# The second float32r part of each weight unit made by an accumulating DMA instead of a subtraction, in a two-layer hybrid decoder trunk

## The chip, the cores and the metric

The kernel runs on one core of a Trainium2 chip. The metric is the time of one execution on the device in microseconds (us), as the median of several runs. The engines go by their short names in the profile: PE (TensorE matmuls; PEld its weight loads), DVE (VectorE), ACT (ScalarE), POOL (GpSimd) and SP (SyncE, which here only issues DMAs). A DMA issued by an engine goes into that engine's queue, and the core's 16 DMA engines carry it out.

## The reference

Two decoder layers over 512 tokens of 1024 features, all in float32. Each layer is a half-step SwiGLU feed-forward, a token mixer, and a second half-step feed-forward; each of these sublayers has an RMS norm before and after it. The mixer of the first layer is a diagonal complex state-space model (S5), that of the second a convolution module of 31 taps.

```
for i in range(DEPTH):                       # DEPTH = 2
    h = swiglu(rmsnorm(x, norm_pre[i, 0]), w1[i, 0], w3[i, 0], w2[i, 0])
    x = x + 0.5 * rmsnorm(h, norm_post[i, 0])
    h = rmsnorm(x, norm_pre[i, 1])
    h = s5_mixer(h, ...) if i == 0 else conv_mixer(h, ...)
    x = x + rmsnorm(h, norm_post[i, 1])
    h = swiglu(rmsnorm(x, norm_pre[i, 2]), w1[i, 1], w3[i, 1], w2[i, 1])
    x = x + 0.5 * rmsnorm(h, norm_post[i, 2])
# swiglu(h) = (silu(h @ w1) * (h @ w3)) @ w2, inner width 2816
```

## The kernel before

**The arithmetic.** PE multiplies in float32r, which keeps fewer bits than float32. So every operand is held as two float32r parts: a first part (the value rounded) and a second part (what the rounding left). A product takes three matmuls: first x first, first x second, second x first (`mm3`, lines 105, 106 and 107, in this order, with the weight's part as the stationary operand). Line 107 is the only one that reads the weight's second part.

**The stream of weights.** All weights are cut into units of 128 x 1024 (512 KB), eight 128 x 128 blocks each: 44 + 22 units for each of four feed-forward sublayers, 24 for each mixer, 312 in all. A unit goes three steps. `w_dma` (line 86) loads it on SP's queue into one of three buffers called raw. `want(n)` splits all units up to n: ACT rounds raw into the first part `hi` (line 97, a cast), and DVE subtracts that from raw into the second part `lo` (line 98). In some places `lo_engine` hands that subtraction to POOL. Then `mm3` uses the unit. 310 units are split by `want`; the first two are split by halves in `start` (lines 188 and 189).

**Buffers and order.** `hi` and `lo` are pages: 39 buffers of 128 x 1024 (tag `pg`), shared with activations and tables. The order of instructions on each engine is the order in which the program emits them; each engine runs its own list in order, and an instruction waits there for the data and buffers that it needs. So the place of a `want` sets how far ahead of its matmuls a unit is split.

- In a feed-forward sublayer (`ffn`) a step takes two units. Step m asks for units up to `u0 + 2m + 4` (`FFN_AHEAD`), behind its own matmuls in the program. At its start, after the entry, `want(u0 + 6)` splits the fifth to seventh unit.
- In a sublayer's last product (`proj`) each unit, when begun, asks for the unit two further on (line 273). Near its end `want(un + 2)` splits the next sublayer's first three units, and while the norm of the first half of the tokens is made, POOL subtracts the fourth, `want(un + 3)`.
- The entry (`entry_step`) runs the next sublayer's first four units, feature tile by feature tile, by halves of the tokens, as the residual and its two parts come from DVE (lines 322, 326, 164) and ACT (lines 154 to 159); POOL adds up the squares (line 160).

**Work beside it.** During the first feed-forward and the next sublayers the tables of the state-space model are made in small portions (queues D, E, Q, K, T, P) on DVE, POOL and ACT. The state-space sublayer and the convolution run mostly on DVE, with a share of POOL and ACT; in the convolution DVE does its taps at line 1037.

Of the kernel before, what the change touches and what calls it, by code (L numbers as in the profile page):

```python
# [7 lines left out]
F32 = mybir.dt.float32  # L8
F32R = mybir.dt.float32r
AF = mybir.ActivationFunctionType  # L10
ALU = mybir.AluOpType
# [3 lines left out]
NF = 22  # L15
EPS_SUM = 1024e-6

# columns of the packed vector input
V_PRE, V_POST, V_BGLU, V_CBIN, V_DWB, V_LNG, V_LNB, V_CBOUT, V_DW = 0, 48, 96, 104, 120, 128, 136, 144, 152
CONV_W = 31  # L20
ND = 9
# taps of a feature tile that the vector engine takes (GpSimd the others), None: the tensor engine
C_TAPS = (31, 0, 21, None, None, None, 20, 16)
NL = 2
S5_ORDER = ("sktwdopcgl", "sktwdopcgl", "stwdopcgkl", "skwtdopcgl", "skwtdopcgl", "skwtdolpcg", "skwtdopcgl", "skwtdopcgl", "skwtdopcgl")
# [14 lines left out]
def trunk(ctx: ExitStack, tc: tile.TileContext, h, plan):  # L40
# [24 lines left out]
    def psum():  # L65
        return psp.tile([P, T], F32, tag="ps", name=nm("ps"))

# [1 line left out]
    x = cpool.tile([P, NK, T], F32, name="x")  # L69
    vec = cpool.tile([P, h["vec"].shape[1]], F32, name="vec")  # L70
    gsc = cpool.tile([P, 96], F32, name="gsc")
# [1 line left out]
    eps = cpool.tile([P, 1], F32, name="eps")  # L73
    lng = cpool.tile([P, 8], F32, name="lng")

# [1 line left out]
    units = [h[name][i] for name, i in plan["units"]]  # L77
    NU = len(units)
    raws, halves = {}, {}
# [10 lines left out]
    def want(n):  # L90
        while ptr["split"] <= min(n, NU - 1):
            u = ptr["split"]
            w_dma(u)
            r = raws.pop(u)
            hi, lo = page(), page()
            hv, lv = hi.rearrange("p a b -> p (a b)"), lo.rearrange("p a b -> p (a b)")
            ACT.copy(hv, r)  # L97
            lo_engine[0].tensor_tensor(lv, r, hv.bitcast(F32), op=ALU.subtract)  # L98
            halves[u] = tuple(v.rearrange("p (k m) -> p k m", m=P) for v in (hv, lv))
            ptr["split"] += 1  # L100
            w_dma(u + 3)
# [4 lines left out]
        PE.matmul(out, lhsT=hi[:, s, :], rhs=xl, start=False, stop=False)  # L106
        PE.matmul(out, lhsT=lo[:, s, :], rhs=xh, start=False, stop=stop)  # L107

# [1 line left out]
    def stat(acc):  # L110
        ps = psum()
        PE.matmul(ps[:, : acc.shape[1]], lhsT=ones, rhs=acc, start=True, stop=True)  # L112
# [37 lines left out]
    HALVES = (slice(0, T // 2), slice(T // 2, T))  # L150

    def split_hi(k, cs, xn, pre, acc2):
        """x[k] times the gain, the first part; the squares of x into acc2."""
        ACT.activation(xn[k][:, 0, cs], x[:, k, cs], AF.Copy, scale=gsc[:, pre + k : pre + k + 1])  # L154
        if k == 0:
            ACT.activation(acc2[:, cs], x[:, k, cs], AF.Square)
        else:
            sq = tmp()
            ACT.activation(sq[:, cs], x[:, k, cs], AF.Square)  # L159
            POOL.tensor_tensor(acc2[:, cs], acc2[:, cs], sq[:, cs], op=ALU.add)  # L160
# [9 lines left out]
            mm3(ps4[j][:, cs], u0 + j, k, xn[k][:, 0, cs], xn[k][:, 1, cs], k == 0, k == NK - 1)  # L170

    def start(pre):
        """The first sublayer's entry."""
        xn = [page() for _ in range(NK)]
        acc2 = stat_tile()
        ps4 = [psum() for _ in range(4)]
        for i in range(11):
            PE.matmul(ps4[2][:, :P], lhsT=ones, rhs=ones, start=True, stop=True)
        pieces = []
        for u in range(2):  # L180
            hi, lo = (flat(page()) for _ in range(2))
            pieces.append((raws.pop(u), hi, lo))
            halves[u] = tuple(v.rearrange("p (k m) -> p k m", m=P) for v in (hi, lo))
        ptr["split"] = 2

        def split_part(u, n):
            r, hi, lo = (v[:, T * n : T * n + T] for v in pieces[u])
            ACT.copy(hi, r)
            DVE.tensor_tensor(lo, r, hi.bitcast(F32), op=ALU.subtract)

        def part_hi(k):
            ACT.activation(xn[k][:, 0, :], x[:, k, :], AF.Copy, scale=gsc[:, pre + k : pre + k + 1])  # L192

        def squares(k):
            if k == 0:
                ACT.activation(acc2, x[:, k, :], AF.Square)
            else:
                sq = tmp()
                ACT.activation(sq, x[:, k, :], AF.Square)
                POOL.tensor_tensor(acc2, acc2, sq, op=ALU.add)  # L200

        for k in range(NK):
            part_hi(k)
            split_lo(k, FULL, xn, pre)
            if k in (0, 4):
                split_part(0, k // 4)
                split_part(1, k // 4)
            entry_step(k, FULL, xn, 0, ps4, (0, 1))
            if k:
                squares(k - 1)  # L210
        want(2)
        squares(NK - 1)
        want(3)
        for j in (2, 3):
            for k in range(NK):
                entry_step(k, FULL, xn, 0, ps4, (j,))
        return {"xn": xn, "ps": ps4, "acc2": acc2, "u": 0}
# [4 lines left out]
        rsqrt(ps, e["y"])  # L222

    def proj(u0, nk, rhs, post, nl, pre, xn, bias=None, lead=None):
        """The sublayer's last product, its norm, the residual, and the next one's entry."""
        acc, acc2 = stat_tile(), stat_tile()
        hp = [page(F32) for _ in range(4)]
        hs = [hp[m // 2][:, m % 2, :] for m in range(NK)]
# [40 lines left out]
        for m in range(0 if lead is None else 4, NK - nl):  # L269
            ps = psum()  # L270
            for k in range(nk):
                if k == 0 or unit(m, k)[1] == 0:
                    want(min(unit(m, k)[0] + 2, un - 1))
                product(m, k, ps, FULL)
                if k == 1 and pend:
                    evac(*pend)
                    copy(*pend)
                if k % 8 == 4:
                    pump("P")
            pend = m, ps, FULL  # L280
# [18 lines left out]
        for i, (m, k) in enumerate((m, k) for m in last for k in range(nk)):  # L299
            if i == 5:  # L300
                sa = stat(acc[:, A])
                steps = rsqrt_steps(sa, y[:, A])
                if pre is not None:
                    lo_engine[0] = POOL
                    want(un + 3)
                    lo_engine[0] = DVE
                for f in steps:
                    f()
            if k == 0:
                psb[m] = psum()[:, :n]  # L310
            product(m, k, psb[m], B)
            if k == nk - 1 and m != NK - 1:
                evac(m, psb[m], B)
                copy(m, psb[m], B)
# [90 lines left out]
        evac(*pend)  # L405
        return proj(u0 + 2 * NF, NF, g, post, 1, pre, g[:NK])

# [1 line left out]
    # A pair is two groups (32 features, 128 complex states). Tokens go in chunks of four: the  # L409
    # stacked input of a chunk is (token in the chunk, feature of the pair) on the partitions.  # L410
    # Of each chunk come its own outputs (M) and its contribution to the state (P); the state
    # runs over the chunks in a frame that turns with it, and gives the rest of the outputs (Q).
    if any(k == "s5" for k, _ in plan["subs"]):
        drp = ctx.enter_context(tc.tile_pool(name="drp", bufs=1, space=bass.MemoryType.DRAM))
        tab_d = drp.tile([8, P, 3584], F32, name="tab_d")
# [3 lines left out]
        m4 = cpool.tile([P, 32], F32, name="m4")  # L419

    def s5_params(tb, F):
        """Per state: powers of abar and of the turn of a chunk, f abar^(3-t)."""
        scr = [page(F32).rearrange("p a (b n) -> p (a b) n", n=32) for _ in range(2)]
        ident = tmp()[:, :P]
        prm = tmp()[:, :96]
# [168 lines left out]
        bg["K"].append(turned())  # L594

    def s5_turn(tb):
        """exp(i phi c) of 128 chunks: 16 of them for all pairs, then tile by tile."""
        H = page(F32).rearrange("p r (q c) -> p r q c", c=16)
        w = page(F32).rearrange("p r (q c) -> p r q c", c=16)
        DVE.memset(H[:, 0, :, 0:1], 1.0)  # L600
# [24 lines left out]
            nc.sync.dma_start(out=tab_d[i, :, 2048:3072], in_=flat(E.rearrange("p r q c -> p r (q c)")))  # L625

    def s5_in():
        """P of the four pairs of each tile."""
        M, A, S = ALU.mult, ALU.add, ALU.subtract

        def load(i):
# [19 lines left out]
            yield  # L651

    def s5_ops(tb, F):
        """Q and M of the four pairs of each tile."""
        M, A, S = ALU.mult, ALU.add, ALU.subtract
        Fv = F.rearrange("p (t i r q) -> p t i r q", t=4, i=8, r=2)
        quads = lambda z: z.rearrange("p (q k g) -> p q k g", q=4, k=4)
# [85 lines left out]
    def s5(e, post, pre):  # L743
# [34 lines left out]
                    PE.matmul(b[:, j, :], lhsT=p[:, r, j, :], rhs=mu[:, 1, j, :], start=True, stop=True)  # L778

        def decay(i):  # L780
            """The coefficients of the scan: |abar|^4, and 0 where a pair begins."""
            if i <= 7:
                cf[i] = stat_tile()
                ACT.copy(quad(cf[i])[:, :, 1:], m4[:, 4 * i : 4 * i + 4].unsqueeze(2).to_broadcast([P, 4, n]))
                POOL.memset(quad(cf[i])[:, :, 0:1], 0.0)
# [102 lines left out]
        for s in range(9):  # L888
# [5 lines left out]
                g4.extend(psum() for _ in range(4))  # L894
            if s:
                back(s - 1)
            # transfers
            y_out(s - 2)
            load(s + 2, (0,))
            unstack(s + 2)  # L900
# [58 lines left out]
            u0 + 16, NK, z, post, NL, pre, [page() for _ in range(NK)], lead=lambda s: (FULL, s) if s < NK else None  # L959
        )  # L960

# [1 line left out]
    # Tiles of 128 features go different ways: on the vector engine (D), on the scalar engine and  # L963
    # GpSimd (G), on both (X), or on the tensor engine with banded operators (T).
    if any(k == "conv" for k, _ in plan["subs"]):
        drc = ctx.enter_context(tc.tile_pool(name="drc", bufs=1, space=bass.MemoryType.DRAM))
        z_d = drc.tile([8, P, T], F32, name="z_d")
# [2 lines left out]
    def conv(e, post, pre):  # L970
# [72 lines left out]
            yield  # L1043

        def diagonals():
            """Taps of the last tiles on the tensor engine, one diagonal matrix each."""
            for i, z, n, m in diags:
                op = flat(page(F32))
                nc.sync.dma_start(out=op[:, : m * P], in_=h["diag"][i - 6, :, n * P : (n + m) * P])
# [36 lines left out]
                total(i, a, b, DVE)  # L1086

        def shifted(i):
            """The tile less the shift, which the first tile's mean gives, and its squares."""
            if i == 0:  # L1090
                ps = psum()
                PE.matmul(ps, lhsT=ones, rhs=cs[0], start=True, stop=True)
                fin.append(lambda: shift(ps))
            fin.append(lambda: sums_of(i))
# [125 lines left out]
        while fin:  # L1220
            finish()
            add_sums()
        # layer norm, by halves of the tokens
        q, v, y0, w = tmp(), tmp(), tmp(), tmp()
        yp = page(F32)
        y, my = yp[:, 0, :], yp[:, 1, :]
# [48 lines left out]
            u0 + 16, NK, rhs, post, NL, pre, [page() for _ in range(NK)], bias=vec[:, V_CBOUT : V_CBOUT + 8], lead=lead  # L1275
        )

# [1 line left out]
    DVE.memset(ones, 1.0)  # L1279
    DVE.memset(eps, EPS_SUM)  # L1280
    nc.scalar.dma_start(out=vec[:, :48], in_=h["vec"][:, :48])
# [138 lines left out]
```

## Time and profile before

| what | value |
|---|---|
| three runs | 2028.13, 2026.94, 2029.37 us; median 2028.13 |
| span of the profiled execution | 2030.4 us; no other time is given for that execution |
| PE busy | 1887.8 us, 93% |
| DVE, ACT, POOL busy | 1267.2, 649.1, 389.4 us |
| mean granted clock of PE | 0.961 of full speed |
| subtractions of line 98 | 295 on DVE at 1261 ns, 15 on POOL at 2479 ns |
| moved by DMA | 229.17 MB, 34.0% of 16 engines' span on SP's queue |

Busy time is the time in which an engine had an instruction running; matmuls overlap, so a busy PE is not a PE at its peak. In a row of groups the two times behind the bar are the busy time of the whole group and the mean of one. "<-" behind an idle time names what ended it. PEclk is the clock that PE was granted, as a share of full speed. The bytes and the time of a DMA queue count what its packets took on the 16 DMA engines together.

### The profile page before, as it was taken

What the parts mean: (1) busy time and instruction counts of PE and PEld (TensorE: products, weight loads), DVE (VectorE), ACT (ScalarE), POOL (GpSimd) and SP (SyncE); (2) the same over time, 40 slices, a digit from 0 to 9 for tenths busy, and PEclk for the clock granted to TensorE, in tenths of its full rate; (3) what the DMA queues carried; (4) which work ended last, traced back from release to release, by engine and by line L of the source; (5) the groups of instructions that cost most, each with busy time, mean ns of one, the idle gap of its engine ahead of it and who ended that gap; (6) DMA issues with size and microseconds to landing.
All of it is one profiled execution on the core that took longest, in us unless ns stands there. A gap on an engine that the chain in (4) does not pass through costs nothing.

```text
span 2030.4 us, 23976 instructions
## 1 busy us (share of the span) xinstructions
PE 1887.8 (93%) x9226; PEld 1591.0 (78%) x9226; DVE 1267.2 (62%) x1828; ACT 649.1 (32%) x939; POOL 389.4 (19%) x401
## 2 busy tenths in 40 slices
PE   9978799998799999999999999999884799999997
PEld 7856588887678888888888888889772788888886
DVE  5998976758965754442376444237999786444324
ACT  4222232233224432222244222224433544232211
POOL 2446533034630100000020000002563120000000
PEclk9988899999899999999999999999996899999999
DMA  4234446846722232323224232231442024332231
GB/s 151 94 107 136 126 135 207 255 167 233 243 75 93 67 124 90 104 76 101 86 71 135 94 104 83 83 106 51 164 142 70 11 73 135 104 97 91 73 114 43
DMA packets 95811, 229.17 MB, mean 113 GB/s; under 512 B 25552, under 2 KB 39376, under 8 KB 95696
## 3 DMA queue, kind: packets, MB, share of 16 engines
q1 hardware_dynamic: 94400, 226.56, 34.0%
q8 instruction: 72, 1.18, 0.2%
q10 hardware_dynamic: 1296, 1.07, 0.2%
q14 instruction: 43, 0.35, 0.1%
HBM read 204.92 MB, written 22.68 MB: 112 GB/s over the span
## 4 chain that ended last, share of the span: by engine, by line
PE 73%; DVE 20%; issue 2%; ACT 2%; DMA 1%; SPq 0%; POOL 0%; DVEq 0%; ACTq 0%; POOLq 0%
PE ps L106 24%; PE ps L107 24%; PE ps L105 23%; DVE pg L1037 3%; DVE pg L98 2%; DVE pg L436 1%; DVE pg L803 1%; PE ps L1142 1%; DVE x L326 1%; DVE tmp L322 1%; DVE pg L164 1%; DVE pg L813 1%; DVE pg L705 1%; DVE pg L706 1%; PE ps L112 0%
## 5 line engine op out<-in xcount | busy, mean ns | idle before, releaser
L107 PE MATMUL ps<-pg,pg 128*128 128x512 f32 (+1 forms) x2808 | 1038.9, 370 | 27.8 <-DVE pg L98 24.7
L105 PE MATMUL ps<-pg,pg 128*128 128x512 f32 (+1 forms) x2808 | 1044.7, 372 | 14.6 <-ACT pg L154 5.0
L106 PE MATMUL ps<-pg,pg 128*128 128x512 f32 (+1 forms) x2808 | 1042.8, 371 | 13.2 <-DVE pg L164 10.0
L107 PEld LDWEIGHTS ps<-pg,pg 128*128 128x128 f32 x2808 | 537.6, 191 | 119.3 <-DVE pg L98 28.6
L106 PEld LDWEIGHTS ps<-pg,pg 128*128 128x128 f32 x2808 | 537.1, 191 | 112.2 <-DVE pg L164 17.4
L105 PEld LDWEIGHTS ps<-pg,pg 128*128 128x128 f32 x2808 | 537.3, 191 | 103.8 <-ACT pg L154 5.4
L98 DVE TENSOR_TENSOR pg<-raw,pg 128x1024 fp32r<-128x1024 f32 x295 | 360.9, 1261 | 84.5 <-ACT pg L97 51.9
L97 ACT CAST pg<-raw 128x1024 fp32r<-128x1024 f32 x310 | 310.1, 1047 | 113.2 <-DMA raw<-w 24.7
L98 POOL TENSOR_TENSOR pg<-raw,pg 128x1024 fp32r<-128x1024 f32 x15 | 36.9, 2479 | 875.3 <-ACT pg L97 875.3
L369 DVE TENSOR_TENSOR tmp<-ps,y 128x512 f32<-128x512 f32 x88 | 60.4, 686 | 217.0 <-PE ps L107 217.0
L248 DVE TENSOR_TENSOR acc<-acc,tmp 128x512 f32<-128x512 f32 (+1 forms) x50 | 36.6, 733 | 228.8 <-ACT tmp L243 228.5
L368 ACT ACTIVATE tmp<-tmp 128x512 f32<-128x512 f32 x88 | 55.6, 632 | 287.0 <-DVE tmp L367 287.0
L372 ACT CAST pg<-tmp 128x512 fp32r<-128x512 f32 x88 | 54.6, 621 | 290.1 <-DVE tmp L370 290.1
L243 ACT ACTIVATE tmp<-ps 128x512 f32<-128x512 f32 (+1 forms) x41 | 21.8, 533 | 267.4 <-PE ps L107 267.1
L1037 DVE SCALAR_TENSOR_TENSOR pg<-pg,vec,pg 128x512 f32<-128x512 f32 x80 | 105.7, 1389 | 0.0
L373 DVE TENSOR_TENSOR pg<-tmp,pg 128x512 fp32r<-128x512 f32 x88 | 61.2, 696 | 64.1 <-ACT pg L372 64.1
L1073 POOL TENSOR_TENSOR pg<-pg,pg 128x512 f32<-128x512 f32 x45 | 73.9, 1642 | 64.9 <-ACT pg L1071 62.0
L160 POOL TENSOR_TENSOR acc<-acc,tmp 128x256 f32<-128x256 f32 x70 | 55.4, 791 | 86.7 <-ACT tmp L159 85.9
L370 DVE TENSOR_TENSOR tmp<-tmp,tmp 128x512 f32<-128x512 f32 x88 | 61.8, 702 | 10.5 <-ACT tmp L368 2.7
L164 DVE SCALAR_TENSOR_TENSOR pg<-x,gsc,pg 128x256 fp32r<-128x256 f32 (+1 forms) x88 | 64.4, 738 | 1.7 <-ACT pg L192 1.6
L154 ACT ACTIVATE pg<-x,gsc 128x256 fp32r<-128x256 f32 x80 | 40.8, 509 | 72.4 <-DVE x L326 72.3
L367 DVE TENSOR_TENSOR tmp<-ps,y 128x512 f32<-128x512 f32 x88 | 60.2, 684 | 3.4 <-PE ps L107 2.7
(172 smaller groups left out, 1223.4 us busy)
## 6 DMA issues: line engine op xcount, KB each, us to landing
raw<-w SPq DMA_DIRECT2D x262, 512.0 KB, 3.9
pg<-tab_d SPq DMA_DIRECT2D x24, 512.0 KB, 6.3
tab_d<-pg SPq DMA_DIRECT2D x16, 512.0 KB, 3.6
raw<-cv_w_in SPq DMA_DIRECT2D x16, 512.0 KB, 4.0
pg<-toep SPq DMA_DIRECT2D x12, 512.0 KB, 6.6
pg<-s5b SPq DMA_DIRECT2D x8, 512.0 KB, 7.4
pg<-f_d SPq DMA_DIRECT2D x32, 128.0 KB, 7.2
raw<-s_w_in SPq DMA_DIRECT2D x8, 512.0 KB, 4.2
```

The costliest lines, as they stand in the source:

```text
L97: ACT.copy(hv, r)
L98: lo_engine[0].tensor_tensor(lv, r, hv.bitcast(F32), op=ALU.subtract)
L105: PE.matmul(out, lhsT=hi[:, s, :], rhs=xh, start=start, stop=False)
L106: PE.matmul(out, lhsT=hi[:, s, :], rhs=xl, start=False, stop=False)
L107: PE.matmul(out, lhsT=lo[:, s, :], rhs=xh, start=False, stop=stop)
L164: DVE.scalar_tensor_tensor(xn[k][:, 1, cs], x[:, k, cs], g, xn[k][:, 0, cs].bitcast(F32), op0=ALU.mult, op1=ALU.subtract)
L367: DVE.tensor_tensor(a, pa, y, op=ALU.mult)
L369: DVE.tensor_tensor(b, pb, y, op=ALU.mult)
L370: DVE.tensor_tensor(a, a, b, op=ALU.mult)
L373: DVE.tensor_tensor(t[:, 1, :], a, t[:, 0, :].bitcast(F32), op=ALU.subtract)
L1037: DVE.scalar_tensor_tensor(a, v, dw(i, w), a, op0=M, op1=A)
L1073: POOL.tensor_tensor(acc, acc, a, op=A)
```

## The change

The second part is no longer a subtraction. ACT, which already rounds the unit into `hi`, makes a second pass over raw with the scale -1, into `lo`, so that `lo` holds the negated first part. Then a DMA on POOL's queue reads the weight a second time from memory and adds it onto `lo`. In `proj` a unit now asks for the unit three further on, not two. `lo_engine` is still set in two places but no longer read.

```
             hi, lo = page(), page()
             hv, lv = hi.rearrange("p a b -> p (a b)"), lo.rearrange("p a b -> p (a b)")
             ACT.copy(hv, r)
-            lo_engine[0].tensor_tensor(lv, r, hv.bitcast(F32), op=ALU.subtract)
+            ACT.activation(lv, r, AF.Copy, scale=-1.0)
+            POOL.dma_start(out=lv, in_=units[u], accum_op=ALU.add)
...
                 if k == 0 or unit(m, k)[1] == 0:
-                    want(min(unit(m, k)[0] + 2, un - 1))
+                    want(min(unit(m, k)[0] + 3, un - 1))
...
                 if pre is not None:
-                    lo_engine[0] = POOL
                     want(un + 3)
-                    lo_engine[0] = DVE
```

Comments go too, and line numbers behind line 98 move by one: the negation is line 98, the DMA line 99, and `mm3` has lines 106 to 108.

Three places show what moves. The first is ACT's list at the entry from the third sublayer into the fourth, both feed-forward (`pg` are pages, `raw` the loaded units, `tmp` and `ps` scratch and accumulators; the numbers are buffers). Before:

```order
L154 ACTIVATE pg_5991<-x,gsc 128x256
L159 ACTIVATE tmp_8016<-x 128x256
L97 CAST pg_8045<-raw_7551 128x1024
L97 CAST pg_8051<-raw_7557 128x1024
L97 CAST pg_8057<-raw_7657 128x1024
L118 ACTIVATE tmp_8083<-ps_8080,eps 128x512
```

Now:

```order
L155 ACTIVATE pg_6100<-x,gsc 128x256
L160 ACTIVATE tmp_8174<-x 128x256
L97 CAST pg_8203<-raw_7707 128x1024
L98 ACTIVATE pg_8204<-raw_7707 128x1024
L97 CAST pg_8210<-raw_7714 128x1024
L98 ACTIVATE pg_8211<-raw_7714 128x1024
L97 CAST pg_8217<-raw_7815 128x1024
L98 ACTIVATE pg_8218<-raw_7815 128x1024
L119 ACTIVATE tmp_8244<-ps_8241,eps 128x512
```

Each cast of a fifth, sixth or seventh unit is now followed by a negation, ahead of the norm's square root. The second is POOL's list at the same place, the last sums of squares of the entry and what stands behind them, now:

```order
L161 TENSOR_TENSOR acc_7062<-acc_7062,tmp_8156 128x256
L161 TENSOR_TENSOR acc_7062<-acc_7062,tmp_8174 128x256
L99 DMA pg_8204<-w_3 128x1024
L99 DMA pg_8211<-w_3 128x1024
L99 DMA pg_8218<-w_3 128x1024
```

Before, POOL had the sums alone here:

```order
L160 TENSOR_TENSOR acc_6927<-acc_6927,tmp_7998 128x256
L160 TENSOR_TENSOR acc_6927<-acc_6927,tmp_8016 128x256
L98 TENSOR_TENSOR pg_10239<-raw_10130,pg_10238 128x1024
```

(the subtraction in the last row belongs to the end of the fourth sublayer). The third is DVE's list in the stretch in which the tables are made; lines 367 to 370 are a feed-forward step's gate. Before:

```order
L719 TENSOR_TENSOR pg_1208<-pg_403,pg_1079 128x128
L720 TENSOR_TENSOR pg_1208<-pg_1208 128x128
L98 TENSOR_TENSOR pg_1291<-raw_1027,pg_1290 128x1024
L98 TENSOR_TENSOR pg_1297<-raw_1154,pg_1296 128x1024
L367 TENSOR_TENSOR tmp_1302<-ps_1096,y_344 128x512
L369 TENSOR_TENSOR tmp_1303<-ps_1097,y_344 128x512
```

Now:

```order
L718 TENSOR_TENSOR pg_1229<-pg_408,pg_1098 128x128
L719 TENSOR_TENSOR pg_1229<-pg_1229 128x128
L366 TENSOR_TENSOR tmp_1325<-ps_1115,y_349 128x512
L368 TENSOR_TENSOR tmp_1326<-ps_1116,y_349 128x512
```

The two subtractions between the table work and the gate are gone from DVE's list.

More of the change, by code (lines that the diff above doesn't have):

```diff
@@ L97, in want @@
             ACT.copy(hv, r)
-            lo_engine[0].tensor_tensor(lv, r, hv.bitcast(F32), op=ALU.subtract)
+            ACT.activation(lv, r, AF.Copy, scale=-1.0)
+            POOL.dma_start(out=lv, in_=units[u], accum_op=ALU.add)
             halves[u] = tuple(v.rearrange("p (k m) -> p k m", m=P) for v in (hv, lv))
@@ L272, in proj @@
                 if k == 0 or unit(m, k)[1] == 0:
-                    want(min(unit(m, k)[0] + 2, un - 1))
+                    want(min(unit(m, k)[0] + 3, un - 1))
                 product(m, k, ps, FULL)
@@ L303, in proj @@
                 if pre is not None:
-                    lo_engine[0] = POOL
                     want(un + 3)
-                    lo_engine[0] = DVE
                 for f in steps:
```

## The prediction

> **What bounds the kernel now.** I read the page's engine table first, then PE's waits, then the busy times by stage, and last the timeline at the places where a second part is waited for.
>
> ```profile
> span 2030.4 us, 23976 instructions
> PE 1887.8 (93%) x9226; PEld 1591.0 (78%) x9226; DVE 1267.2 (62%) x1828; ACT 649.1 (32%) x939; POOL 389.4 (19%) x401
> L98 DVE TENSOR_TENSOR pg<-raw,pg 128x1024 fp32r<-128x1024 f32 x295 | 360.9, 1261 | 84.5 <-ACT pg L97 51.9
> L97 ACT CAST pg<-raw 128x1024 fp32r<-128x1024 f32 x310 | 310.1, 1047 | 113.2 <-DMA raw<-w 24.7
> L98 POOL TENSOR_TENSOR pg<-raw,pg 128x1024 fp32r<-128x1024 f32 x15 | 36.9, 2479 | 875.3 <-ACT pg L97 875.3
> ```
>
> The matmuls fill 93% of the span, so the 310 subtractions (361 us of VectorE, 37 of GpSimd) are mostly hidden. What they can cost is PE's idle time, 2030.4 - 1887.8 = 143 us, and the clock lost after it. Where is it? Busy time by stage, and then line 98 alone in the same three stages:
>
> ```profile
> 100.00:250.00 150.00, 117.18 (x498) 92.87 (x497) 137.15 (x292) 36.65 (x53) 81.26 (x115) 0.86 0.40 122
> 475.00:580.00 105.00, 82.42 (x456) 72.36 (x455) 98.98 (x94) 19.10 (x29) 68.78 (x55) 0.87 0.68 231
> 1425.00:1590.00 165.00, 116.03 (x563) 94.87 (x562) 160.64 (x152) 66.76 (x97) 94.81 (x57) 0.84 0.32 110
> 750.00:1000.00 250.00, 250.00 (x1105) 207.08 (x1104) 98.44 (x115) 64.62 (x80) 0.00 (x0) 1.00 0.28 91
> ```
>
> ```profile
> 100.00:250.00 150.00, 22.38 (x16) 0.46 (x1) 0.86 0.40 122
> 475.00:580.00 105.00, 17.06 (x10) 0.00 (x0) 0.87 0.68 231
> 1425.00:1590.00 165.00, 18.39 (x13) 0.00 (x0) 0.84 0.32 110
> ```
>
> The columns are the stretch, PE, weight loads, DVE, ACT, POOL, the granted clock and the DMA share (in the second fence DVE and POOL only). Three stretches (table preparation, state-space sublayer, convolution) are DVE's: it is busy 91 to 97%, PE idles 33, 23 and 49 us, and the clock is 0.84 to 0.87. In the feed-forward stretch in the fourth row PE is full, a matmul takes 250/1105 = 0.226 us, and a unit of 24 takes 5.4 us.
>
> **What is removed.** *Preparation.* PE's waits between 100 and 250 us:
>
> ```profile
> PE ps L107 <- DVE pg L98: 19.0, 6, 6.5
> PE ps L583 <- DVE pg L577: 6.7, 1, 6.7
> ```
>
> DVE is the queue there, and 22.4 us leave it; PE also stops waiting for second parts behind DVE's table work. The ends are 22 (DVE's time alone) and 33 (all of PE's idle time); I take 28. *Convolution.* 18.4 us leave a DVE that is busy 160.6 of 165; the ends are 0 and 18, I take 18, since DMA is at 0.32 and POOL at 57%. *State space.* 17.1 us leave DVE, but DMA is at 0.68 of 105 = 71 us there and gets ten more transfers (priced below at 3.2 us, so 103 of 105). The ends are -17 and +14 (at 4.8 us each); I take -5.
>
> *Sublayer ends.* Five of POOL's subtractions stand here, while DVE makes the norm:
>
> ```profile
> 1022.21 2.62 POOL L98 TENSOR_TENSOR pg<-raw,pg 128x1024 fp32r<-128x1024 f32 x1 [337.16 <-ACT pg L97]
> 1022.60 2.84 DVE L322 TENSOR_TENSOR tmp<-pg,y 128x256 f32<-128x256 f32 x2
> 1025.76 0.41 DVE L322 TENSOR_TENSOR tmp<-pg,y 128x256 f32<-128x256 f32 x1
> ```
>
> DVE's two products take 2.84 where two take 0.82: POOL's subtraction holds DVE up for 2.0 us, on the path to the next entry. Five times 2.0 is 10. After the state-space and convolution sublayers PE's wait there also costs clock:
>
> ```profile
> PE ps L105 <- ACT pg L154: 5.0, 2, 2.5
> 658.80:665.70 6.90, 6.21 (x29) 5.91 (x29) 4.65 (x10) 2.06 (x6) 2.45 (x4) 0.51 0.01 2
> 665.70:672.60 6.90, 6.02 (x45) 5.36 (x44) 5.84 (x13) 2.92 (x7) 1.65 (x3) 1.00 0.00 1
> ```
>
> The 2.5 us wait ends at 657.1; the next 6.9 us run at 0.51, so about 3.4 us of matmul time go. Twice 3.4 is 7, gained if these waits shrink to half a us. Removed in all: 28 + 18 + 5 + 10 + 7 = 68.
>
> The Trainium skill, "SBUF — State Buffer" (Who interferes with whom), says a DVE instruction with two SBUF inputs contends with a GpSimd instruction that reads SBUF and not with one that only writes. By that rule the 2.84 us row is agreed with, and an issue on POOL, which reads no tensor, would hold up nothing, so the 10 stays whole; if an issue blocked DVE as the subtraction does, the sum below would be 10 worse. No row of this case shows an issue on POOL.
>
> **What is added.** *ACT:* 310 negations. The nearest row is line 97's, 1.05 us, so 325 us; ACT goes from 649 to 974, 48%, and where PE is full it is hidden: the second parts of a step are made 22 us ahead.
>
> ```profile
> 800.24 2.36 DVE L98 TENSOR_TENSOR pg<-raw,pg 128x1024 fp32r<-128x1024 f32 x2 [0.26 <-ACT pg L97]
> 807.94 0.69 DVE L369 TENSOR_TENSOR tmp<-ps,y 128x512 f32<-128x512 f32 x1 [4.74 <-PE ps L107]
> ```
>
> At 807.9 PE ends a step; the two units split at 800 are the fourth and fifth from there, needed at 807.9 + 3 x 5.4 = 824. In the last products the change of 2 to 3 in the look-ahead adds a unit, 16 us instead of 11. Not hidden: three negations stand ahead of the squares at the ends of the state-space and convolution sublayers, where the norm then comes some 1.5 us later; twice, 3.
>
> *DMA engines:* each accumulation reads the weight again, reads the negated part and writes it.
>
> ```profile
> q1 hardware_dynamic: 94400, 226.56, 34.0%
> 325.00:425.00 100.00, 99.02 (x437) 81.67 (x436) 61.92 (x82) 23.78 (x28) 17.52 (x34) 1.00 0.77 238
> ```
>
> A plain 0.524 MB costs 0.340 x 2030 x 0.524/226.56 = 1.6 us of all 16 engines. That is the low end; three plain transfers, 4.8, are the high one. I take two, 3.2, one for each source. Where PE is full the share goes from 0.28 to 0.28 + 3.2/5.4 = 0.87: it fits. Between 325 and 425 it is 77 + 18 x 3.2 = 135 us of work in 100. The lead of 16 to 22 us covers most of the 35 over, in part twice, since the queue drains where the tables do; I take 10, ends 0 and 35.
>
> The Trainium skill, "Collectives: The Full Stack" (The bandwidth ceiling), says an adding transfer moves at half the rate of a copy because it needs two source reads (measured 1.93). By it the price would be about 3.1 us, by the nearest row as it stands 1.6, with which 10 would be 0 to 3 and the state-space term nearer 17. No run here shows it.
>
> *Landing time X,* from POOL's free issue to the semaphore:
>
> ```profile
> raw<-w SPq DMA_DIRECT2D x262, 512.0 KB, 3.9
> pg<-s5b SPq DMA_DIRECT2D x8, 512.0 KB, 7.4
> ```
>
> Bounds 3.9 and 7.4; I take 6.0, the quiet 3.9 with one more reading of 1.6 and half a us to issue. It matters where there is no lead, at the first units after each entry:
>
> ```profile
> 1050.94 2.93 ACT L97 CAST pg<-raw 128x1024 fp32r<-128x1024 f32 x3
> 1051.17 0.88 POOL L160 TENSOR_TENSOR acc<-acc,tmp 128x256 f32<-128x256 f32 x1 [0.40 <-ACT tmp L159]
> 1052.00 2.36 DVE L98 TENSOR_TENSOR pg<-raw,pg 128x1024 fp32r<-128x1024 f32 x2 [0.55 <-ACT pg L97]
> 1054.61 0.39 PE L107 MATMUL ps<-pg,pg 128*128 128x512 f32 x1
> ```
>
> Now DVE's part is ready at 1053.2, and PE wants it at 1054.6. Then: first part 1052.0, negated 1053.0, POOL is free (its add ends 1052.05), landing 1053.0 + X = 1059.0. Stall X - 1.6 = 4.4, at five entries 22. Such a gap costs clock as above: 3.4 at four of them (at the convolution's DVE is the bound) is 14. The units behind land in time: 2.1 us apart, needed 5.4 apart. The unit that POOL subtracted (split from 1021.1 on, ACT's cast at 1.04 and the negation to 1023.2) lands at 1029.2 and is wanted about 3 us sooner; DVE paces that half entry, so I take 1 of 3, five times, 5. At the start the third unit's issue stands behind six of POOL's adds:
>
> ```profile
> 13.09 8.11 POOL L200 TENSOR_TENSOR acc<-acc,tmp 128x512 f32<-128x512 f32 x5 [0.33 <-ACT tmp L199]
> ```
>
> The sixth of seven ends near 20, the part lands at 26, PE wants it near 23: 3, and 3 of clock. 6.
>
> *POOL:* 310 issues, behind its own work in order; the adds of squares, the table products and the taps queue behind each, and each waits for ACT. POOL is at 81 of 150 us in preparation. At half a us it hides; at the 2.5 of its subtraction it would be 81 + 27 x 2.5 = 149.
>
> **Sum.** Added 3 + 10 + 22 + 14 + 5 + 6 = 60, removed 68: -8 on the profiled 2030.4, which is 2.3 above the median of the runs, 2028.1. So 2020.
>
> **Rivals.** *Slow landing (other side).* Each us of X costs 5 at the entries, up to 4 at the half entries, 1 at the start. From X = 7 it cancels the gain; at X = 9 it is -8 + 30 = +22, 2050. For it: the 7.4 row, in a busy stretch; against: entries are quiet. *DMA engines the bound.* At 4.8 us a unit takes 1.6 + 4.8 = 6.4 against 5.4: some 250 feed-forward units times 0.9 is +225, with lead lost everywhere; from about 3.8 it begins, and at 4.1 it is 0.3 x 250 = 75, 2100. For it: 0.77 and 0.68 already; against: 0.28 in most of the span. *More is gained.* X near 4, 33 and 17 in the first and second stages: 33 + 18 + 17 + 17 = 85 less 12 + 7 + 3 + 3 + 5 = 30, 1973. For it: 19 us of PE's waits name line 98. *POOL the bound.* At 2.5 us an issue preparation gives back some 20: 2040.
>
> **Chances.** My case 0.46 (2005 to 2030), slow landing 0.20, more gained 0.17, DMA bound 0.11, POOL 0.06. Change under 0.2% (4 us) is about what a measurement of this kernel can't tell from none. Of my case 0.29 lies below 2024, 0.09 within 4 us, 0.08 above: faster 0.29 + 0.17 = 0.46, same 0.09 + 0.01 = 0.10, slower 0.08 + 0.20 + 0.11 + 0.05 = 0.44. The range leaves out half of "more gained" below and the DMA bound above: 1978 to 2085.
>
> **What would show it.** Right: PE's waits on line 98 gone between 100 and 250 us; DVE near 905 us; L322 at 0.41 everywhere at the ends; PE waiting 4 to 5 us at line 108 (the third matmul) once after each entry, and for nothing in the feed-forward middles. Wrong: accumulations landing over 7 us after issue, DMA share near 1 where PE was full, PE waiting for second parts there, or POOL's issue taking us rather than half of one.

## The result, and the profile after

The change made the kernel slower: 2153.78 us (median, 2138.45 to 2160.82) against 2028.75 for the kernel before on the same chip, a ratio of 1.0601 [1.0561, 1.0641]. Forecast were 2020 us and a range of 1978 to 2085. The profiled execution took 2152.92 us, with a span of 2151.1. From its page:

```profile
span 2151.1 us, 24707 instructions
PE 1918.6 (89%) x9226; PEld 1610.5 (75%) x9226; DVE 888.7 (41%) x1533; ACT 944.5 (44%) x1249; POOL 608.1 (28%) x696
q0 software_dynamic: 44640, 162.55, 40.2%
L99 POOL DMA_DIRECT2D pg<-w x262 | 227.6, 874 | 1128.2 <-ACT pg L98 1020.4
raw<-w SPq DMA_DIRECT2D x262, 512.0 KB, 8.3
pg<-w POOLq DMA_DIRECT2D x262, 512.0 KB, 9.3
```

VectorE lost its 360.9 us of subtractions and a little more (1267.2 to 888.7). The span grew by 120.7 us all the same: PE's idle time by 89.9 (from 142.6 to 232.5), and PE's busy time by 30.8 for the same 9226 matmuls, which is lost clock (0.945 against 0.961). The last two rows point to the cause. An adding DMA lands 9.3 us after its issue (median), where 6.0 was assumed, and the plain loads beside it now take 8.3 where they took 3.9. PE's waits show who feels it (us in total, times, longest):

```profile
PE ps L108 <- DMA pg<-w: 98.2, 25, 7.9
PE ps L108 <- DMA pg<-s_w_in: 15.7, 4, 7.5
PE ps L108 <- DMA pg<-cv_w_in: 15.6, 4, 6.5
PE ps L108 <- DMA pg<-s_w_out: 14.2, 5, 6.0
```

These four rows hold 143.7 us. Line 108 is the third matmul, the only reader of a second part. Where are they? First the entry from the third sublayer into the fourth, then the first steps behind it:

```profile
1104.80 0.58 PE L108 MATMUL ps<-pg,pg 128*128 128x256 f32 x1 [2.87 <-DMA pg<-w]
1129.86 1.05 ACT L98 ACTIVATE pg<-raw 128x1024 fp32r<-128x1024 f32 x1
1131.21 0.88 POOL L99 DMA_DIRECT2D pg<-w  x1 [1.16 <-PE ps L108]
1140.65 0.80 PE L108 MATMUL ps<-pg,pg 128*128 128x512 f32 x1 [7.92 <-DMA pg<-w]
1158.45 0.86 POOL L99 DMA_DIRECT2D pg<-w  x1 [22.60 <-DVE tmp L368]
1165.62 0.79 PE L108 MATMUL ps<-pg,pg 128*128 128x512 f32 x1 [5.43 <-DMA pg<-w]
```

The first row is the entry's fourth unit, 2.9 us late. The next three are the fifth: negated at 1129.9, issued at 1131.2, used at 1140.7, so X, from issue to use, is 9.4 us, and PE stands for 7.9. The last two are the eighth unit, which the prediction did not list: its split stands behind the first two gates (lines 365 to 371), which wait for the norm, so it is issued at 1158.5 and wanted at 1160.2.

The prediction called the entries quiet. The DMA engines do stand still before the split, at a share of 0.01 from 1121 to 1131 us. But each of the three negations also frees a loaded unit's buffer, so six transfers of 512 KB are issued within 4 us: three plain loads (at 1130.9, 1132.8 and 1134.7 us, each behind its negation) and three adding DMAs. While the first adding one is under way the share is 0.90. In the first fence are that stretch and the six issues; in the second the last two adding DMAs of the kernel, which no load accompanies:

```profile
1131.20:1140.70 9.50, 1.58 (x12) 1.15 (x11) 0.00 (x0) 3.50 (x4) 2.61 (x3) 0.69 0.90 213
raw<-w SPq DMA_DIRECT2D x3, 512.0 KB, 8.3
pg<-w POOLq DMA_DIRECT2D x3, 512.0 KB, 11.4
```

```profile
pg<-w POOLq DMA_DIRECT2D x2, 512.0 KB, 5.9
```

The last two landed in 5.4 and 6.4 us. So 6.0 was a fair price for an adding DMA with little beside it, and not for one in such a burst.

The stages, cut where ACT takes the square root of a norm (line 118 before, 119 after), against the forecast's terms:

| stage | forecast | measured | PE's waits on adding DMAs there |
|---|---|---|---|
| start | +6 | +5.2 | 6.7 |
| five entries | +27 (22 + 14 + 5 + 3 - 10 - 7) | +65.8 | 55.2 |
| first sublayer, behind its start | -18 (10 - 28) | +9.4 | 39.2 |
| state space | -5 | +21.8 | 19.7 |
| convolution | -18 | -6.6 | 9.2 |
| three later feed-forwards | 0 | +9.9, +7.3, +7.4 | 7.3, 5.4, 4.9 |
| sum | -8 | 120.2 of the 120.7 | 147.6 |

Busy times by stretch (columns as in the prediction: PE, weight loads, DVE, ACT, POOL, clock, DMA share, GB/s), first two of the kernel before, then those of the changed kernel. The share adds up the times of all packets over the time of 16 engines; where it passes 1, packets overlap:

```profile
40.00:100.00 60.00, 58.84 (x259) 48.26 (x258) 52.30 (x126) 17.85 (x22) 23.36 (x10) 1.00 0.23 77
250.00:325.00 75.00, 75.00 (x348) 62.70 (x347) 52.38 (x83) 23.18 (x32) 24.24 (x45) 1.00 0.41 132
```

```profile
40.00:100.00 60.00, 55.08 (x229) 44.68 (x228) 38.07 (x164) 32.73 (x38) 9.56 (x12) 0.94 0.72 184
100.00:250.00 150.00, 134.45 (x621) 111.21 (x621) 117.14 (x257) 51.33 (x68) 96.67 (x137) 0.95 0.77 188
250.00:325.00 75.00, 67.28 (x292) 55.23 (x291) 28.19 (x54) 35.48 (x45) 36.59 (x65) 0.93 0.84 209
325.00:425.00 100.00, 89.02 (x365) 71.90 (x364) 37.90 (x59) 35.86 (x40) 15.58 (x19) 0.93 1.04 281
498.00:700.00 202.00, 162.61 (x816) 136.99 (x814) 107.11 (x122) 72.42 (x94) 81.42 (x76) 0.89 0.69 200
800.00:1000.00 200.00, 200.00 (x884) 165.62 (x883) 47.07 (x68) 90.02 (x107) 30.95 (x37) 1.00 0.80 186
```

The gain in preparation did come: 621 matmuls between 100 and 250 us instead of 498 (506 instead of 398 of them with weights, the others for the tables), at 0.226 us each 24 to 28 us. It was lost again ahead of that stretch (229 instead of 259) and behind it (292 and 365 instead of 348 and 437). The feed-forward middles (last row) run as before, 0.226 us a matmul, with ACT's pass and DMA at 0.80 hidden.

### The profile page after: what moved, and what is told of

Read it like the earlier page. It is cut to its first block, busy times and chain, and to the rows that moved or that the text cites. A ratio compares the mean times of both kernels' runs of the same rounds, so it can differ in the third digit from the quotient of the medians.

```text
span 2151.1 us, 24707 instructions
## 1 busy us (share of the span) xinstructions
PE 1918.6 (89%) x9226; PEld 1610.5 (75%) x9226; DVE 888.7 (41%) x1533; ACT 944.5 (44%) x1249; POOL 608.1 (28%) x696
## 4 chain that ended last, share of the span: by engine, by line
PE 55%; issue 11%; DMA 10%; DVE 10%; ACT 3%; POOL 2%; SPq 0%; POOLq 0%; DVEq 0%; ACTq 0%
PE ps L108 18%; PE ps L107 18%; PE ps L106 18%; DMA pg<-w 5%; DVE pg L1036 4%; DMA pg<-s_w_in 1%; ACT pg L98 1%; DMA tab_d<-pg 1%; DMA pg<-cv_w_in 1%; DVE pg L165 1%; ACT pg L97 1%; DVE x L325 1%; DVE pg L802 1%; DMA u_d<-tmp 1%; DVE tmp L321 0%
## 5 line engine op out<-in xcount | busy, mean ns | idle before, releaser
L108 PE MATMUL ps<-pg,pg 128*128 128x512 f32 (+1 forms) x2808 | 1058.3, 377 | 148.6 <-DMA pg<-w 98.2
L106 PE MATMUL ps<-pg,pg 128*128 128x512 f32 (+1 forms) x2808 | 1056.1, 376 | 7.1 <-ACT pg L1267 4.4
L107 PE MATMUL ps<-pg,pg 128*128 128x512 f32 (+1 forms) x2808 | 1052.3, 375 | 7.0 <-DVE pg L165 5.9
L108 PEld LDWEIGHTS ps<-pg,pg 128*128 128x128 f32 x2808 | 546.8, 195 | 254.1 <-DMA pg<-w 107.6
L107 PEld LDWEIGHTS ps<-pg,pg 128*128 128x128 f32 x2808 | 545.6, 194 | 107.1 <-DVE pg L165 11.8
L106 PEld LDWEIGHTS ps<-pg,pg 128*128 128x128 f32 x2808 | 547.1, 195 | 96.3 <-ACT pg L1267 4.8
L99 POOL DMA_DIRECT2D pg<-w x262 | 227.6, 874 | 1128.2 <-ACT pg L98 1020.4
L97 ACT CAST pg<-raw 128x1024 fp32r<-128x1024 f32 x310 | 322.4, 1040 | 91.7 <-DMA raw<-w 31.8
L98 ACT ACTIVATE pg<-raw 128x1024 fp32r<-128x1024 f32 x310 | 327.1, 1055 | 78.3 <-PE ps L107 43.4
L249 DVE TENSOR_TENSOR acc<-acc,tmp 128x512 f32<-128x512 f32 (+1 forms) x50 | 31.4, 628 | 342.1 <-ACT tmp L244 341.9
L367 ACT ACTIVATE tmp<-tmp 128x512 f32<-128x512 f32 x88 | 55.2, 627 | 55.9 <-DVE tmp L366 55.9
L121 DVE SCALAR_TENSOR_TENSOR tmp<-tmp 128x256 f32<-128x256 f32 (+1 forms) x18 | 9.3, 515 | 148.6 <-ACT tmp L119 148.6
```

The source lines that it names most:

```text
L98: ACT.activation(lv, r, AF.Copy, scale=-1.0)
L99: POOL.dma_start(out=lv, in_=units[u], accum_op=ALU.add)
L106: PE.matmul(out, lhsT=hi[:, s, :], rhs=xh, start=start, stop=False)
```

## The experiments

The theory after the result was **lead**: an adding DMA costs nothing where its unit is split 12 us or more ahead of its use, and up to its landing, some 9 us, where it is not. The main rival was **throughput**: the doubled DMA work or ACT's extra pass slows everything. Medians stand against 2030.08 us (runs 1, 3, 4 and 5), 2031.32 (runs 2, 6, 9 and 10) and 2030.14 (runs 7, 8 and 11) for the kernel before.

**1. Short-lead units subtracted.** 52 of the 310 units go the old way, 258 by DMA, and POOL again takes the fourth unit's subtraction. Subtracted are the first seven of each feed-forward sublayer (in the first of them two are the start's, which the 54 of the expectation count), and the first six (eight for `cv_w_in`) of `s_w_in`, `s_w_out`, `cv_w_in` and `cv_w_out`.

```
-            ACT.activation(lv, r, AF.Copy, scale=-1.0)
-            POOL.dma_start(out=lv, in_=units[u], accum_op=ALU.add)
+            if u in SHORT:
+                lo_engine[0].tensor_tensor(lv, r, hv.bitcast(F32), op=ALU.subtract)
+            else:
+                ACT.activation(lv, r, AF.Copy, scale=-1.0)
+                POOL.dma_start(out=lv, in_=units[u], accum_op=ALU.add)
```

> 54 of the 310 units go back to the subtraction: in each feed-forward sublayer the first seven, in the state-space sublayer 0-5 and 16-21 of its 24, in the convolution 0-7 and 16-21. These are the units that are split less than about 12 us before PE needs them. Theory 'lead' (the accumulation takes about 9 us to land even in quiet, and costs only where there is no lead): the five entries, which grew by 66 us in all between the two norms, go back; so does the start (5) and most of what follows the entries and of the two mixers' output products (30). Expected 2154 - 100 = 2055, range 2035 to 2070, with PE's waits for accumulated parts below 50 us instead of 148. Theory 'throughput' (the DMA engines at 72% make every part late): 54 of 310 less is 17% of the 125 us, so about 2130.

Measured: 2061.05 us, ratio 1.0155 [1.0138, 1.0172]. 52 of 310 units carried three quarters of the loss; as a price on every unit, throughput is out. What remained, first PE's waits of this kernel:

```profile
PE ps L112 <- DMA pg<-w: 60.7, 15, 9.6
```

and from its timeline the eighth unit of the third sublayer:

```profile
712.40 0.87 POOL L103 DMA_DIRECT2D pg<-w  x1 [17.84 <-DVE tmp L374]
721.52 0.80 PE L112 MATMUL ps<-pg,pg 128*128 128x512 f32 x1 [7.04 <-DMA pg<-w]
```

The three later feed-forwards were still 7.5 to 9.5 us longer each, the first sublayer 10.3.

**2. More subtracted.** As 1, and the whole first sublayer and the eighth and ninth unit of the later feed-forwards too.

```
-SHORT = {b + i for b in (0, 90, 156, 246) for i in range(7)} | ...
+SHORT = set(range(66)) | {b + i for b in (90, 156, 246) for i in range(9)} | ...
```

> As the version with the short-lead units subtracted, but also the whole first sublayer (units 0 to 65) and the eighth and ninth unit of the three later feed-forward sublayers are subtracted again. Some 160 units of feed-forward middles, state space and convolution still go by the adding DMA. Theory 'lead': what the short-lead version still lost (31 us) was lost at two kinds of places, the eighth unit of each feed-forward sublayer (split behind two gates that wait for the norm, about 8 us each with its clock, three times 8 = 24) and the first sublayer (10): both go, 2026 (2016 to 2036). Rival 'throughput': DMA at 0.8 of its time in the feed-forward middles, or ACT's extra pass, costs time of its own: 2045 or more.

Measured: 2023.24 us, ratio 0.9965 [0.9953, 0.9977]. The three feed-forwards are back at 329.1 us each, as before the change, while DMA works at 0.79 in their middles (busy times by stretch, then what is left of PE's waits on second parts):

```profile
800.00:1000.00 200.00, 200.00 (x884) 165.62 (x883) 34.80 (x51) 83.17 (x97) 31.17 (x36) 1.00 0.79 187
```

```profile
PE ps L112 <- DVE pg L100: 18.1, 6, 5.5
PE ps L112 <- DMA pg<-cv_w_in: 6.7, 1, 6.7
PE ps L112 <- DMA pg<-s_w_in: 4.1, 1, 4.1
```

So the loss lies in units with too little lead: this kernel still issues 193 adding DMAs, which land in 9.0 us (median), and PE waits for six of them, 15.4 us in all, the two longest shown. Only in the first sublayer, where the changed kernel's DMA engines are at 1.04 for 100 us, lead and throughput were not told apart.

**3. The look-ahead of three alone,** in the kernel before.

```
-                    want(min(unit(m, k)[0] + 2, un - 1))
+                    want(min(unit(m, k)[0] + 3, un - 1))
```

> The kernel before with the look-ahead of 3 instead of 2 in the last products, and nothing else. The subtraction is ready well before it is wanted there, so 'lead' expects no change: 2028, within 4 us. If holding one more unit's two pages starves the tables of pages, it would cost some 10 us, and that share of the loss would belong to the look-ahead.

Measured: 2026.46 us, ratio 0.9985 [0.9975, 0.9995]: not the cause, 3 us better if anything.

**4. The negation alone.** ACT makes the negated part, and DVE (or POOL) adds the loaded unit onto it; no DMA.

```
-            lo_engine[0].tensor_tensor(lv, r, hv.bitcast(F32), op=ALU.subtract)
+            ACT.activation(lv, r, AF.Copy, scale=-1.0)
+            lo_engine[0].tensor_tensor(lv, r, lv.bitcast(F32), op=ALU.add)
```

> The kernel before with ACT's negation added and the subtraction replaced by adding raw onto it on the same engine; no DMA. It prices ACT's 310 extra passes (325 us busy). 'Lead' and 'throughput' both expect little: the second part comes 1.05 us later, felt at five entries and twice ahead of a norm, 5 to 15 us, so 2035 to 2043. A third theory, that ACT's longer list is what delays the rest, expects 2080 or more.

Measured: 2040.32 us, ratio 1.0062 [1.0047, 1.0077]. ACT's pass costs about 10 us by the medians, 9.5 to 15.6 by the interval of the ratio. The feed-forwards keep their 329.1 us; state space is 3.5 longer and the convolution 3.3, but 1.5 of the 3.5 also stand in the profiles of runs 3, 9 and 10, which leave the state space alone.

**5. The entry's units ahead.** In the changed kernel the fifth and sixth unit are split with the fourth, during the norm.

```
-                    want(un + 3)
+                    want(un + 5)
```

> The changed kernel, with the next sublayer's fifth and sixth unit asked for two units sooner: at the norm at the end of the last product, together with the fourth, and not after the entry. 'Lead': the wait of about 8 us for the fifth unit after each entry goes, with its clock (3.4), so five times 11 = 55 comes back; but two more casts and negations (4.2 us) stand ahead of the entry's first parts on ACT, of which some 2 to 4 us are felt, five times. Net -35 to -45: 2110 to 2120. 'Throughput' expects no gain: the parts are as late as before, 2150 or more.

Measured: 2110.62 us, ratio 1.0411 [1.0392, 1.0429]: 43 us better than the changed kernel, as lead forecast. Among PE's waits those on second parts shrink, and a new one comes, on the residual's first parts, which stand behind the splits on ACT:

```profile
PE ps L108 <- DMA pg<-w: 61.9, 16, 7.5
PE ps L106 <- ACT pg L155: 25.0, 5, 8.0
```

**6. A plain copy.** POOL's DMA copies and does not add, so the second part holds the whole weight.

```
-            POOL.dma_start(out=lv, in_=units[u], accum_op=ALU.add)
+            POOL.dma_start(out=lv, in_=units[u])
```

> The changed kernel, but POOL's DMA copies the weight over the negated first part and does not add it; the adding is left out, so the second part holds the whole weight. Same queue, same issues, same order, same negations. Theory 'adding': the changed kernel is slow because an adding transfer takes twice the time of a plain one on the DMA engines (327 against 159 ns for a packet of 4096 bytes) and lands in 9.3 us. A plain one then lands in about 5 to 6 us, and the stalls where there is no lead shrink by about 4 us each at some 30 places and their lost clock with them: 2050 (2035 to 2080). Rival 'queue': the landing comes from POOL's queue (issue 0.87 us and a fixed time behind it), not from adding: it stays at 8 us or more and the time over 2120.

Measured: 2040.23 us, ratio 1.0054 [1.0025, 1.0082]; the forecast of 2050 held, the queue did not. The same queue with the same issues, without adding, on the page, among PE's waits, and at the entry into the fourth sublayer:

```profile
q0 software_dynamic: 44640, 162.55, 22.7%
pg<-w POOLq DMA_DIRECT2D x262, 512.0 KB, 5.9
```

```profile
PE ps L108 <- DMA pg<-w: 38.4, 13, 5.0
```

```profile
1048.71 0.57 POOL L99 DMA_DIRECT2D pg<-w  x1 [1.17 <-PE ps L108]
1053.20 0.50 PE L108 MATMUL ps<-pg,pg 128*128 128x512 f32 x1 [2.94 <-DMA pg<-w]
```

Adding itself is worth 2153.8 - 2040.2 = 114 us of the loss. At the same entry X is 4.5 us, not 9.4, with the same six transfers. The last two units, without loads beside them, landed in 3.9 and 4.8 us here and in 5.4 and 6.4 in the changed kernel. A plain unit takes 0.227 x 2037.1 / 310 = 1.49 us of all 16 DMA engines, an adding one 0.402 x 2151.1 / 310 = 2.79, a factor of 1.87.

**7. Halves.** The changed kernel, each adding DMA issued as two of 256 KB.

```
-            POOL.dma_start(out=lv, in_=units[u], accum_op=ALU.add)
+            for c in (slice(0, 512), slice(512, 1024)):
+                POOL.dma_start(out=lv[:, c], in_=units[u][:, c], accum_op=ALU.add)
```

> The changed kernel, but each adding DMA is issued as two of 256 KB, first the half that holds the first four of the unit's eight blocks; bytes, order and lead are the same. Theory 'the transfer's own time stalls PE': the first half lands about 3 us before the whole did (9.3), the second half is wanted 2.7 us later, so each of some 27 stalls shrinks by 2 to 3 us with its clock: 2075 (2050 to 2110). Rival 'fixed cost and issue': POOL's issue of 0.87 us is paid twice and packets of 2048 bytes take as long as those of 4096, so DMA work doubles: 2150 or more.

Measured: 2127.89 us, ratio 1.0492 [1.0457, 1.0526]: better than the changed kernel by 26, not by the 80 expected, and neither theory's number. PE's waits, the page's queue, and the same entry:

```profile
PE ps L109 <- DMA pg<-w: 60.6, 17, 5.4
```

```profile
q0 software_dynamic: 89280, 162.57, 43.9%
```

```profile
1114.30 5.53 POOL L100 DMA_DIRECT2D pg<-w  x6 [1.17 <-PE ps L109]
1120.00 0.47 PE L109 MATMUL ps<-pg,pg 128*128 128x512 f32 x1 [4.16 <-DMA pg<-w]
```

At the entry it works: the first half is used 5.7 us after its issue, and the stall there falls from 7.9 to 4.2. DMA work does not double (0.439 x 2120.4 / 310 = 3.00 us a unit against 2.79). In all, the waits on adding DMAs fall from 147.6 to 100.9 us. Not all of it is gained: three waits of the same matmul, 13.0 us, are new and put down to ACT's rows. That leaves 34, and the profiled span fell by 30.7.

**8. The old look-ahead of two in the changed kernel.** The edit of 3, the other way round.

> The changed kernel with the old look-ahead of two units in the last products. Theory 'lead': a unit is then asked for two units of 5.4 us = 10.9 us ahead; cast and negation take 2.1 and the landing 9.3, 11.4 in all, so each unit of the four feed-forward last products, of 16 to 22 units, stalls PE 0.5 to 1 us, and the later ones partly hide behind the stalls before: some 40 to 90 us more, 2215 (2190 to 2245). Rival 'order alone': the list runs ahead as far as the buffers allow whatever the look-ahead says, within 10 us of the changed kernel, 2144 to 2164.

Measured: 2150.04 us, ratio 1.0592 [1.0567, 1.0617], as the changed kernel. The number is the rival's, but the list did not run ahead whatever the look-ahead says. In the fourth feed-forward's last product, from its fourth unit on, the distance from issue to first use is 10 to 20 us here and 12 to 25 in the changed kernel (the unit's use counted off by the order of the third matmuls). ACT makes the splits there mostly in threes, each three behind a square of the product before, for which it waits:

```profile
2032.45 0.60 ACT L244 ACTIVATE acc<-ps 128x512 f32<-128x512 f32 x1 [8.96 <-PE ps L108]
pg<-w POOLq DMA_DIRECT2D x1, 512.0 KB, 7.0
```

The second row is the first issue of the next three, at 2035.2 us: it landed in 7.0 and was used after 9.7, the shortest distance there. So the look-ahead does set the lead. The lead theory's sum failed because the units with the shortest lead are the first of three, which land in about 7 us and not in the median's 9.3.

**9. Preparation only.** The kernel before with units 13 to 34 by negation and adding DMA (`if u not in PREP:` ahead of the subtraction, `else` as in 1).

> The kernel before with one part of the change: units 13 to 34, those that run while the tables are prepared (100 to 250 us), get negation and adding DMA; all else as before. Theory 'the preparation gain is real': DVE is the queue there, and the short-lead version was 115 matmuls (26 us) further in that stretch, before it lost them again between 250 and 435 us where DMA was at 1.0. Without adding transfers behind 250 us the gain stays: 2010 (2003 to 2018), ratio 0.990. Rival 'the gain is given back': the faster first sublayer only runs into the table work and transfers of 250 to 435 us (DMA 0.67 to 0.84 there already) and the sublayer's end comes at the same time: 2024 to 2032.

Measured: 2017.74 us, ratio 0.9935 [0.9923, 0.9948], half way between the two theories. Busy times by stretch, and the first unit by DMA:

```profile
40.00:100.00 60.00, 51.34 (x218) 42.00 (x218) 51.14 (x170) 25.35 (x32) 19.54 (x12) 0.91 0.45 126
100.00:250.00 150.00, 134.14 (x616) 110.82 (x615) 118.16 (x254) 53.83 (x71) 95.78 (x136) 0.94 0.78 194
```

```profile
90.80 0.80 PE L112 MATMUL ps<-pg,pg 128*128 128x512 f32 x1 [8.66 <-DMA pg<-w]
```

The gain in the stretch is 616 - 498 = 118 matmuls, 102 of them with weights, 23 to 27 us. The first unit that goes by DMA has no lead and stalls PE for 8.7 us, which takes 259 - 218 = 41 matmuls, 9 us, from the stretch before (259 is the kernel before's count there). Of the 14 to 18 left, the sublayer keeps 14.4 behind its start.

**10. Convolution only.** The same with the eight units 230 to 237.

> The kernel before with one part of the change: the eight units 230 to 237 in the convolution's middle get negation and adding DMA; all else as before. DVE is busy 97% of that stretch and loses eight subtractions of 1.26 us = 10 us. Theory 'DVE bounds the convolution': 2020 (2016 to 2024). Rival 'PE's own units set the end': no change within 4 us, 2026 to 2032.

Measured: 2020.11 us, ratio 0.9949 [0.9936, 0.9961]. DVE bounds the convolution: eight subtractions of 1.26 us are 10, and 11.2 are gained by the medians (the stage is 9.1 shorter in the profile), though here too the first unit by DMA comes late, among PE's waits:

```profile
PE ps L112 <- DMA pg<-cv_w_in: 6.3, 1, 6.3
```

**11. What gained, combined:** 9 and 10 and the look-ahead of three in the kernel before.

```
+BY_DMA = set(range(13, 35)) | set(range(230, 238))
...
+            if u not in BY_DMA:
                 lo_engine[0].tensor_tensor(lv, r, hv.bitcast(F32), op=ALU.subtract)
+            else:
+                ACT.activation(lv, r, AF.Copy, scale=-1.0)
+                POOL.dma_start(out=lv, in_=units[u], accum_op=ALU.add)
...
-                    want(min(unit(m, k)[0] + 2, un - 1))
+                    want(min(unit(m, k)[0] + 3, un - 1))
```

> The kernel before with the parts of the change that gained: units 13 to 34 (preparation) and 230 to 237 (convolution) by negation and adding DMA, and the look-ahead of 3 in the last products; all other units subtracted. The parts lie in different stages. Theory 'the parts add up': 13.6 (preparation alone) + 11.2 (convolution alone) + 3.1 (look-ahead alone) = 28 below before, 2003 (1998 to 2008). Rival 'they share a slack': a later stage gives part of it back, 2010 to 2018.

Measured: 2002.49 us (2000.83 to 2007.15), ratio 0.9874 [0.9857, 0.9891]. The parts add up. It beats both kernels, with 30 adding DMAs instead of 310.

## Why the prediction was wrong

Between the forecast and the measured stages lie 128 us: 39 at the entries, 27 in the first sublayer, 27 in the state space, 25 in the later feed-forwards and 11 in the convolution, less 1 at the start.

**The landing time is the step that failed first.** "I take 6.0" (bounds 3.9 and 7.4) holds for an adding DMA with little beside it, 5.4 and 6.4 at the kernel's end. It was put where six transfers start at once, on the ground that "entries are quiet", and there X was 9.4; the median of all is 9.3, and "over 7 us after issue" was one of the prediction's signs of being wrong. The formula stood: "stall X - 1.6" gives 7.8, and PE waited 7.9. That case was the rival "slow landing", with 2050 at X = 9. It came out 100 us above this, because the second failure is larger.

**Where there is no lead was counted short.** The prediction priced the landing at the entries' fourth and fifth unit and at the start.
- *Fifth unit with its clock:* 36 forecast, 44.7 measured (growth from the first half's norm to the whole one, five entries).
- *Third and fourth unit:* "I take 1 of 3" gave 5 for the fourth and nothing for the third, and with ACT's 3 and the gains of 10 and 7 the first half of the entries was to shrink by 9; it grew by 21.2. PE waited 21.4 us for these two units, up to 3.2 at once, and the clock fell where it was to recover, to 0.58 in the stretch below. VectorE's product (line 321 now) did get faster, but by 45.5 - 41.1 = 4.4 us in all, not 10: before, only three of the five ends had a slow one (2.5 us), and 0.95 us of each is left:

```profile
1104.80:1112.00 7.20, 7.20 (x36) 7.08 (x37) 0.29 (x1) 0.48 (x1) 0.29 (x1) 0.58 0.01 3
L322 DVE TENSOR_TENSOR tmp<-pg,y 128x256 f32<-128x256 f32 x96 | 45.5, 479 | 0.3
L321 DVE TENSOR_TENSOR tmp<-pg,y 128x256 f32<-128x256 f32 x96 | 41.1, 433 | 0.3
```

- *Feed-forwards,* priced at nothing under "the second parts of a step are made 22 us ahead". True of the middles, false of the eighth unit, whose split stands behind the gates: 24.6 in three sublayers. Run 2 took this away by subtracting two units more.
- *State space:* -5 forecast, +21.8 measured, and for a wrong reason. The prediction feared the DMA engines, but their share is 0.69; PE waits 19.7 us there for second parts, 14.2 of them of `s_w_out`. With half of its units subtracted (run 1) the stage is 2.0 longer than before, with plain copies 1.7, against 1.5 in kernels that leave it alone. So no run shows a gain, either, from the 17.1 us that leave DVE in this stage.

**Preparation** was right in its stretch, 28 forecast and 24 to 28 measured. What failed is that the stretch stands between two that give it back: a first unit without lead (9 us in run 9), and the stretch from 250 to 425 us, in which PE did 128 matmuls fewer, up to 29 us. The prediction had 135% of the DMA engines' time there from 325 us on, at a cost of 10; the share was 1.04, and the term was about a third of the loss. With plain copies (run 6) the sublayer is 15.9 us shorter than before. In the changed kernel it is 9.4 us longer than before; with DMAs for units 13 to 34 alone (run 9) 14.4 shorter.

**Convolution:** 18 forecast, for 13 subtractions; 6.6 in the changed kernel and 11.2 for eight units alone. The mechanism was right for these eight. But with plain copies for all units, where PE's waits on second parts are 5.3 us in the stage, it is only 8.5 shorter, so 18 was too much even without adding; what else bounds the stage was not tried.

**ACT** was 3 and is about 10 (run 4): the pass is hidden in the feed-forwards, not wholly in the mixers.

**Right were** the DMA engines' price (3.2 forecast, 2.79 measured), hence that feed-forward middles would fit at 0.87 (0.80) and the DMA bound would not come there. The start (+6, +5.2) was near by luck: PE waited 6.7 us and not 3, and the starts of kernels that leave it alone lie from 36.1 to 40.3 us. POOL's issue was half a us and is 0.87; no wait above names it. The Trainium skill's page "Collectives: The Full Stack" (The bandwidth ceiling) has a collective's adding step at half the rate of its copying step, because it reads two sources (measured 1.93); run 6's 1.87 agrees.

The Trainium skill's page "DMA: Bandwidth & Descriptors" (Anatomy of one DMA — SWDGE (gpsimd) path) gives a transfer issued from GpSimd about 2.0 us plus its bytes over 436 GB/s, an estimate of 3.2 us for 512 KB. Without loads beside them the plain copy took 3.9 and the adding one 5.4, at the entry 4.5 and 9.4: the measurement decides, and neither the page's sum nor that sum with its variable part doubled (4.4) would have given the adding one.

## What to carry to other kernels

Work moved from an engine to a DMA trades busy time for latency: before summing what the engine gains, list every place where the operand is wanted sooner after its making than the transfer lands (entries, first units behind a gate, the first unit of a stretch), ask what else is issued there in the same few microseconds, and leave those on the engine. Use the move where the relieved engine is the bound, here 30 units of 310, and measure that stretch's gain against the first unit's stall. A look-ahead in the program is a place in a list, not a time: what the list waits for in between decides, and the lead is read from the trace as the distance from an issue to its use.

## What was not expected of the hardware

- An adding DMA takes 1.87 times a copy's time on the DMA engines, and what that does to its landing depends on what runs beside it: 5.4 against 3.9 us without loads, 9.4 against 4.5 at an entry, as the first of three beside three loads. That the company makes the difference is read from these traces; no run separates it. In the last products of run 8 the first of three, beside three loads too, landed in 7.0; why the entry's took longer is open.
- POOL's issue of an adding 512 KB transfer takes 874 ns, of a plain one 535:

```profile
L99 POOL DMA_DIRECT2D pg<-w x262 | 140.1, 535 | 1147.2 <-ACT pg L98 1048.9
```

- A second stream slows the first: the plain loads' median landing was 3.9 us before, 5.1 beside plain copies and 8.3 beside adding ones.
